# Nine modulation vectors as row products: transposed weights times a spread c, summed by VectorE, loaded by GpSimd's queue

## The chip, the cores and the metric

One core of a Trainium2 chip runs the whole kernel. The metric is the device time of one execution in microseconds; of several executions the median is given. The engines are TensorE (matrix products, PE in the profile; PEld is its weight load), VectorE (DVE), ScalarE (ACT), GpSimd (POOL) and SyncE (SP, which here only issues transfers). Each has its own queue and takes its instructions in order. Transfers run on 16 DMA engines that all queues share.

## What is computed

A trunk of two layers on 256 positions of width 2048: layer 0 is an RWKV-7 time mixing with a squared-ReLU MLP, layer 1 a chunked band attention with another such MLP. Every sub-layer is modulated by vectors made from one conditioning vector c:

```python
for layer in range(DEPTH):
    mod = c @ w_ada[layer] + b_ada[layer]
    sh1, sc1, gt1, sh2, sc2, gt2 = jnp.split(mod, 6, axis=-1)
    if layer == N_A_LAYERS:
        sh_kv, sc_kv = jnp.split(c @ w_ada_kv + b_ada_kv, 2, axis=-1)
        h_kv = modulate(rms_norm(x, g_kv), sh_kv, sc_kv)
        k_s, v_s = h_kv @ w_k_shared, h_kv @ w_v_shared
    h = modulate(rms_norm(x, g_mix[layer]), sh1, sc1)
    y = rwkv7_time_mix(h, ...) if layer < N_A_LAYERS else chunk_band_attention(h, kp, vp, ...)
    x = x + gt1 * y
    h = modulate(rms_norm(x, g_mlp[layer]), sh2, sc2)
    x = x + gt2 * sq_relu_mlp(h, w_up[layer], w_down[layer])
return rms_norm(x, g_final)
```

There are 6 + 6 + 2 = 14 modulation vectors of 2048 elements, each c (2048) times a matrix of 2048 x 2048: 16 MB of weights for each, read once, two operations for each weight. `(layer, part)` names a vector: parts 0 and 1 are the first shift and scale, 2 the first gate, 3 and 4 the second shift and scale, 5 the second gate; `("kv", 0)` and `("kv", 1)` are the shift and scale of the shared keys and values.

## The kernel before

**Layout.** Activations lie with the feature on the 128 partitions and the 256 positions in the row: `x` is [128, 16, 256]. Vectors lie as [128, 16], a column for each 128 features.

**The large products.** Every weight matrix is taken in blocks of 128 output columns (16 for width 2048). `weight` loads such a block in two halves of [128, 1024] (512 KB each) into `raw` (6 buffers, SP's queue); `halves` cuts each into a rounded part wH (ScalarE, L378) and the rest wL (VectorE, L381), with three buffers of each. `proj2` then takes 16 pairs of products (L412, L413) for a block, into `pj`. Behind a block VectorE adds up the two sums, or adds them to x (L960, L1016, L945).

**The modulation vectors.** (0,0) and (0,1) are made at the start, in a way of their own: the lower half of c as products on TensorE, the upper half as rows, L696, with `crow`, the upper half of c, spread over the partitions. The other twelve are made a step at a time beside the large products, in the order of `ada_tiles`: for each vector two halves of 1024 output columns, for each half 16 tiles of [128, 1024], one for each 128 elements of c, 384 tiles in all. `ada_step` takes one tile: VectorE multiplies it with the c of its partition and adds it to `acc` (L452 for the first, L454 for the other 15; `acc` has one buffer). Behind the 16th, `ada_sum` sums `acc` over the partitions: 32 products with a column of ones on TensorE (L476), and VectorE adds the bias (L480). `fin` runs these right away, as `lazy` is never set.

**When steps are taken.** `ada(n)` takes n steps and then calls `ada_fill`. In the time mixing it is called in three slots of four from the third pair of heads on (111 tiles, loaded into `raw`, one at a time); in the MLPs behind every block, one and two steps in turn (`ada_tick`); in the attention one step behind a key block, two behind a value block, one or two behind a query block; in the attention's output projection one step for each of the first ten blocks. `ada_need` takes whatever is missing when a vector is wanted. In the MLPs and the attention the tiles have a pool of their own, `rada` (`ada_room`: 5 buffers in the MLPs, 3 in the attention), and `ada_fill` keeps one load less than that ahead. All loads, those of `rada` too, are issued from SP's queue (L368), each behind the wait for its buffer.

**Order.** The program is written in one order; a scheduler then places each engine's instructions, by this order and by its own estimate of when each is ready, so that modulation steps may be placed ahead of instructions that were written before them. `tc.issue_after(i)` keeps what is written in its block, on the engine of i, behind i. GpSimd's own work in the later stages is the sum of squares (L518) and the masks of the scores (L1095, L1096).

Of the kernel before, what the change touches and what calls it, by code (L numbers as in the profile page):

```python
# [12 lines left out]
F32 = mybir.dt.float32  # L13
F32R = mybir.dt.float32r
AF = mybir.ActivationFunctionType
ALU = mybir.AluOpType
AX = mybir.AxisListType

P = 128
D = 2048  # L20
T = 256
KT = D // P
# [8 lines left out]
HK = 8  # L31
# [298 lines left out]
class Body:  # L330
# [27 lines left out]
            self.ada_pool = None  # L358

    def raw(self, src, shape=None, ada=False):  # L360
        if ada and self.ada_pool:
            pool, n = self.ada_pool
            t = pool.tile([P, HK * P], F32, tag="rada", bufs=n, name="rada")
        else:
            t = self.wp.tile([P, HK * P], F32, tag="raw", bufs=self.RAW_BUFS, name="raw")
        if shape is not None:
            t = t.rearrange("p (a b) -> p a b", a=shape)
        self.nc.sync.dma_start(out=t, in_=src)  # L368
        return t

    def halves(self, raw, lo=0):
# [47 lines left out]

    def ada_src(self, layer, part):  # L420
        if layer == "kv":
            at, w = 2 * 96 + 16 * part, self.d["w_ada_kv"]
        else:
            at, w = 96 * layer + 16 * part, self.d["w_ada"][layer]
        return w[:, part * D:(part + 1) * D], self.bada[:, at:at + KT]

    def ada_tiles(self):
        for key in [(0, 2), (0, 4), (0, 3), (0, 5), ("kv", 1), ("kv", 0),
                    (1, 1), (1, 0), (1, 2), (1, 4), (1, 3), (1, 5)]:
            for half in range(KT // HK):  # L430
                for kt in range(KT):
                    yield key, half, kt

    def ada_load(self):
        tile_ = next(self.adas, None)
        if tile_ is not None:
            key, half, kt = tile_
            w, n_ = self.ada_src(*key)[0], HK * P
            raw = self.raw(w[kt * P:(kt + 1) * P, half * n_:(half + 1) * n_], ada=True)
            self.ada_q.append((key, half, kt, raw))  # L440
        return tile_ is not None

    def ada_step(self):
        nc = self.nc
        if not (self.ada_q or self.ada_load()):
            return
        key, half, kt, raw = self.ada_q.popleft()
        ck = self.ct[:, kt:kt + 1]
        if kt == 0:
            self.fin(HK)  # L450
# [4 lines left out]
        if kt == KT - 1:  # L455
            self.fins = self.ada_sum(self.acc, self.mods[key], half, self.ada_src(*key)[1])
            if not self.lazy:
                self.fin(HK)
            if half == KT // HK - 1:
                self.ada_done.add(key)  # L460

    def ada_fill(self):
# [22 lines left out]
            next(self.fins, None)  # L485

    def ada(self, n=1):
        for _ in range(n):
            self.ada_step()
        self.ada_fill()  # L490

    def last_pe(self):
        pe = self.nc.tensor.engine
        return next(i for i in reversed(self.nc.cur_bb.bb.instructions) if i.engine == pe)

    def ada_need(self, *keys):
        while not all(k in self.ada_done for k in keys):
# [76 lines left out]
    def run(self):  # L574
        nc, tc, d = self.nc, self.tc, self.d
        ctx = self.ctx
        gp = self.gp = ctx.enter_context(tc.tile_pool(name="gp", bufs=1))
# [14 lines left out]
            self.mods[(0, part)] = self.mods01[:, part, :]  # L592
        self.nhalf, self.pool_every = 0, 0
        self.lazy, self.fins, self.ada_pool = False, iter(()), None
        self.ada_done = set()
        self.adas, self.ada_q = self.ada_tiles(), deque()

# [2 lines left out]
        with ExitStack() as st:  # L600
# [21 lines left out]
            with ExitStack() as s2:  # L622
# [4 lines left out]
                r = self.rstd()  # L627
# [535 lines left out]
def _arrange(x, c, w_ada, b_ada, g_mix, g_mlp, w_up, w_down,  # L1163
# [5 lines left out]
    f = lambda a: np.ascontiguousarray(np.asarray(a))  # L1169
    w_ada = f(w_ada)  # L1170
# [9 lines left out]
    for i, w in ((0, rwkv_w2), (1, rwkv_a2)):  # L1180
        w = f(w)[0]
# [17 lines left out]
        "b_ada": f(np.concatenate([f(b_ada).reshape(-1), f(b_ada_kv).reshape(-1)]).reshape(-1, P).T),  # L1199
        "w_ada0": f(w_ada[0][:HK * P, :2 * D]),  # L1200
        "w_ada0_t": f(w_ada[0][HK * P:, :2 * D].T).reshape(2 * KT, P, HK * P),
        "w_ada": f(w_ada), "w_ada_kv": f(w_ada_kv),
        "w_up": np.stack([_pack(w) for w in f(w_up)]),
        "w_down": np.stack([_pack(w) for w in f(w_down)]),
        "w_r": _pack(f(rwkv_w_r)[0]), "w_k": _pack(f(rwkv_w_k)[0]), "w_v": w_v,
# [26 lines left out]
```

## Time and profile before

| | |
|---|---|
| three runs | 2665.96, 2665.98, 2670.43 us; median 2665.98 |
| profiled execution | 2668.82 us, of which the span of its instructions is 2667.0 us |
| mean granted TensorE clock | 0.992 |
| read from memory | 656.72 MB, 247 GB/s over the span |
| loads into `rada` | 273 of 512 KB |

A page of the profile gives busy times of each engine, the costliest groups of instructions (line, engine, operation, what is written and read, shape, count, busy time and mean), transfers with the time from issue to landing, and waits with what ended them. Rows in order of time begin with the start in us and the duration in us. In the table by stage each engine's busy time stands with the number of its instructions, then the granted clock, the DMA engines' share and GB/s. The stages are, roughly: start and time mixing to 710 us, its output projection to 780, the first MLP to 1515, the attention to 1840, its output projection to 1940, the second MLP to the end.

### The profile page before, as it was taken

Reading aid. Unit: us, or ns where it says so; the run is one execution under the profiler, and the core shown is the slowest. Engines: PE = TensorE matmul, PEld = TensorE weight load, DVE = VectorE, ACT = ScalarE, POOL = GpSimd, SP = SyncE. Lnnn points to the kernel's source line nnn. Section 1 sums busy time; section 2 is a strip of 40 time slices with the busy share of each in tenths; the row PEclk is TensorE's granted clock in tenths of the full one; section 3 lists DMA queues with packets and bytes.
Section 4 is the critical chain, followed back from the end, with each engine's and each line's share of the span. In section 5 each row is a group of like instructions: output and inputs, shape, how many; then the busy total and the mean of one; then the engine's idle time right before and its main releaser. Section 6 shows DMA issues by size and latency. Waiting matters only on the chain.

```text
span 2667.0 us, 58173 instructions
## 1 busy us (share of the span) xinstructions
PE 2594.2 (97%) x23596; PEld 2229.2 (84%) x23596; DVE 2112.8 (79%) x3102; ACT 1345.2 (50%) x2435; POOL 208.7 (8%) x320
## 2 busy tenths in 40 slices
PE   7999999999999999999999999999999999999997
PEld 4787777887899888888888998877898888888886
DVE  6788888889789888888888898899887555555555
ACT  3346455555456445355365554565564463453554
POOL 0002223322110000000001100000100000000002
PEclk9999999999999999999999999999999999999998
DMA  9976556566778888889898679887766555555553
GB/s 349 312 244 211 185 179 207 180 214 199 246 236 312 309 317 327 319 324 332 318 329 293 238 242 331 318 274 256 265 218 235 190 189 184 188 189 186 186 189 119
DMA packets 207149, 662.62 MB, mean 248 GB/s; under 512 B 21408, under 2 KB 54560, under 8 KB 206880
## 3 DMA queue, kind: packets, MB, share of 16 engines
q1 hardware_dynamic: 204816, 656.36, 71.5%
q8 instruction: 185, 3.03, 0.5%
q10 hardware_dynamic: 2064, 2.54, 0.3%
q14 instruction: 84, 0.69, 0.1%
HBM read 656.72 MB, written 2.10 MB: 247 GB/s over the span
## 4 chain that ended last, share of the span: by engine, by line
PE 85%; DVE 5%; issue 4%; DMA 4%; ACT 2%; POOL 1%; DVEq 0%; SPq 0%; ACTq 0%; POOLq 0%
PE pj L412 45%; PE pj L413 23%; PE pj L402 2%; PE pj L401 2%; PE pj L403 2%; DMA raw<-w_ada 1%; DVE wL L381 1%; PE iv L111 1%; DVE acc L454 1%; PE gr L105 1%; ACT wH L378 1%; PE ms L115 1%; PE o L401 1%; PE ms L324 0%; PE ms L105 0%
## 5 line engine op out<-in xcount | busy, mean ns | idle before, releaser
L381 DVE TENSOR_TENSOR wL<-raw,wH 128x1024 fp32r<-128x1024 f32 x772 | 941.1, 1220 | 354.9 <-ACT wH L378 347.0
L378 ACT CAST wH<-raw 128x1024 fp32r<-128x1024 f32 x772 | 805.8, 1045 | 799.7 <-PE pj L412 650.0
L412 PE MATMUL pj<-aHL,wH 128*128 128x512 f32 x3328 | 1202.0, 403 | 1.9 <-DVE x L945 1.4
L413 PE MATMUL pj<-aHL,wL 128*128 128x256 f32 x3328 | 936.1, 281 | 0.4 <-DVE wL L381 0.4
L412 PEld LDWEIGHTS pj<-aHL,wH 128*128 128x128 f32 x3328 | 629.4, 189 | 154.4 <-issue 8.7
L412 PE MATMUL pj<-hHL,wH 128*128 128x512 f32 x2048 | 723.0, 398 | 0.0
L413 PEld LDWEIGHTS pj<-aHL,wL 128*128 128x128 f32 x3328 | 629.4, 189 | 3.1 <-issue 0.8
L413 PE MATMUL pj<-hHL,wL 128*128 128x256 f32 x2048 | 574.4, 281 | 0.0
L412 PEld LDWEIGHTS pj<-hHL,wH 128*128 128x128 f32 x2048 | 384.6, 188 | 94.4 <-DVE hHL L991 0.2
L413 PEld LDWEIGHTS pj<-hHL,wL 128*128 128x128 f32 x2048 | 386.8, 189 | 0.1
L454 DVE SCALAR_TENSOR_TENSOR acc<-rada,ct,acc 128x1024 f32<-128x1024 f32 x256 | 327.2, 1278 | 8.5 <-DMA rada<-w_ada 7.6
L518 POOL TENSOR_TENSOR ss<-ss,sq 128x256 f32<-128x256 f32 x56 | 52.6, 940 | 1590.8 <-ACT sq L517 1590.5
L1016 DVE SCALAR_TENSOR_TENSOR x<-pj,mod,x 128x256 f32<-128x256 f32 x256 | 123.4, 482 | 58.6 <-PE pj L413 54.9
L454 DVE SCALAR_TENSOR_TENSOR acc<-raw,ct,acc 128x1024 f32<-128x1024 f32 x104 | 136.2, 1309 | 15.3 <-DMA raw<-w_ada 14.9
L988 ACT ACTIVATE t<-t 128x256 f32<-128x256 f32 x112 | 46.8, 418 | 123.5 <-DVE t L960 123.5
L401 PE MATMUL pj<-aHL,wH 128*128 128x258 f32 x384 | 109.0, 284 | 0.0
L402 PE MATMUL pj<-aHL,wH 128*128 128x258 f32 x384 | 108.9, 284 | 0.0
L403 PE MATMUL pj<-aHL,wL 128*128 128x258 f32 x384 | 108.0, 281 | 0.0
L403 PEld LDWEIGHTS pj<-aHL,wL 128*128 128x128 f32 x384 | 73.2, 191 | 0.2
L402 PEld LDWEIGHTS pj<-aHL,wH 128*128 128x128 f32 x384 | 72.6, 189 | 0.1
L401 PEld LDWEIGHTS pj<-aHL,wH 128*128 128x128 f32 x384 | 72.2, 188 | 0.2
L990 ACT ACTIVATE t<-t 128x256 f32<-128x256 f32 x128 | 53.4, 417 | 3.4
(249 smaller groups left out, 2815.5 us busy)
## 6 DMA issues: line engine op xcount, KB each, us to landing
raw<-w_up SPq DMA_DIRECT2D x256, 512.0 KB, 4.2
raw<-w_down SPq DMA_DIRECT2D x256, 512.0 KB, 4.3
rada<-w_ada SPq DMA_DIRECT2D x209, 512.0 KB, 5.8
raw<-w_ada SPq DMA_DIRECT2D x111, 512.0 KB, 4.3
rada<-w_ada_kv SPq DMA_DIRECT2D x64, 512.0 KB, 6.1
rawa<-w_ada SPq DMA_DIRECT2D x32, 512.0 KB, 6.9
rawa<-w_ada_t SPq DMA_DIRECT2D x32, 512.0 KB, 7.5
raw<-w_k SPq DMA_DIRECT2D x32, 512.0 KB, 4.0
```

Of the source, the lines that this page charges most:

```text
L378: nc.scalar.copy(Hf, raw)
L381: eng.tensor_tensor(out=Lf, in0=raw, in1=Hf, op=ALU.subtract)
L401: nc.tensor.matmul(ps, H[:, i, :], a(kt)[:, 0, :], start=(first and kt == 0), stop=False)
L402: nc.tensor.matmul(ps, H[:, i, :], a(kt)[:, 1, :], start=False, stop=False)
L403: ins = nc.tensor.matmul(ps, L[:, i, :], a(kt)[:, 0, :], start=False, stop=(last and kt == KT - 1))
L412: nc.tensor.matmul(ps, H[:, i, :], a(kt), start=(kt == 0), stop=False)
L413: ins = nc.tensor.matmul(ps[:, 0, :], L[:, i, :], a(kt)[:, 0, :], start=False, stop=(kt == KT - 1))
L454: nc.vector.scalar_tensor_tensor(out=self.acc, in0=raw, scalar=ck, in1=self.acc, op0=ALU.mult, op1=ALU.add)
L518: (eng or nc.gpsimd).tensor_tensor(out=self.ss, in0=self.ss, in1=sq, op=ALU.add)
L988: nc.scalar.activation(t, t, AF.Relu)
L990: nc.scalar.activation(t, t, AF.Square)
L1016: nc.vector.scalar_tensor_tensor(out=x, in0=ps[:, i, :], scalar=self.mods[(layer, 5)][:, n:n + 1], in1=x, op0=ALU.mult, op1=ALU.add)
```

## The change

Three vectors, (0,2), (0,4) and (0,3), are made as before. The other nine, from (0,5) on, are made from transposed weights (`w_ada_t`, laid out outside the kernel): a tile is 128 output features by one half (1024) of c, contiguous in memory. `ada_row` multiplies it in place with `cb`, that half of c spread over the 128 partitions, and the same VectorE instruction sums the row into one column of the vector, for the first half of c, or of `sums`, for the second. Behind 16 tiles one addition on VectorE adds the bias (first half) or the sums (second half). TensorE takes no part. There are as many tiles as before, 288 for the nine vectors, and the order of the halves is such that `cb` changes its half five times behind the first load: first halves and second halves of several vectors are taken together. `cb` takes the buffer of `acc` and is loaded by SP's queue.

Loads into `rada` are issued from GpSimd's queue instead of SP's; loads into `raw` stay with SP. Where there is a `rada`, `ada` keeps its steps behind the last VectorE instruction written so far.

```diff
--- before.py
+++ after.py
@@ -358,14 +358,16 @@
             self.ada_pool = None
 
     def raw(self, src, shape=None, ada=False):
+        queue = self.nc.sync
         if ada and self.ada_pool:
             pool, n = self.ada_pool
+            queue = self.nc.gpsimd
             t = pool.tile([P, HK * P], F32, tag="rada", bufs=n, name="rada")
         else:
             t = self.wp.tile([P, HK * P], F32, tag="raw", bufs=self.RAW_BUFS, name="raw")
         if shape is not None:
             t = t.rearrange("p (a b) -> p a b", a=shape)
-        self.nc.sync.dma_start(out=t, in_=src)
+        queue.dma_start(out=t, in_=src)
         return t
 
     def halves(self, raw, lo=0):
@@ -419,32 +421,49 @@
 
     def ada_src(self, layer, part):
         if layer == "kv":
-            at, w = 2 * 96 + 16 * part, self.d["w_ada_kv"]
+            at, first = 2 * 96 + 16 * part, KT * (7 + part)
         else:
-            at, w = 96 * layer + 16 * part, self.d["w_ada"][layer]
-        return w[:, part * D:(part + 1) * D], self.bada[:, at:at + KT]
+            at, first = 96 * layer + 16 * part, KT * (1 + part if layer else 0)
+        if layer == 0 and part < 5:
+            w = self.d["w_ada"][:, (part - 2) * D:(part - 1) * D]
+        else:
+            w = self.d["w_ada_t"][first:first + KT]
+        return w, self.bada[:, at:at + KT]
 
     def ada_tiles(self):
-        for key in [(0, 2), (0, 4), (0, 3), (0, 5), ("kv", 1), ("kv", 0),
-                    (1, 1), (1, 0), (1, 2), (1, 4), (1, 3), (1, 5)]:
+        for key in [(0, 2), (0, 4), (0, 3)]:
             for half in range(KT // HK):
                 for kt in range(KT):
-                    yield key, half, kt
+                    yield key, half, kt, None
+        e, f, g = (0, 5), ("kv", 1), ("kv", 0)
+        p, q, r, s, t, u = [(1, i) for i in (1, 0, 2, 4, 3, 5)]
+        seen = set()
+        for half, keys in enumerate([[e], [e, f, g], [f, g, p, q], [p, q, r, s, t], [r, s, t, u], [u]]):
+            for key in keys:
+                for n in range(KT):
+                    yield key, half % 2, n, key in seen
+                seen.add(key)
 
     def ada_load(self):
         tile_ = next(self.adas, None)
         if tile_ is not None:
-            key, half, kt = tile_
+            key, half, kt, last = tile_
             w, n_ = self.ada_src(*key)[0], HK * P
-            raw = self.raw(w[kt * P:(kt + 1) * P, half * n_:(half + 1) * n_], ada=True)
-            self.ada_q.append((key, half, kt, raw))
+            if last is None:
+                raw = self.raw(w[kt * P:(kt + 1) * P, half * n_:(half + 1) * n_], ada=True)
+            else:
+                raw = self.raw(w[kt, half], ada=True)
+            self.ada_q.append((key, half, kt, last, raw))
         return tile_ is not None
 
     def ada_step(self):
         nc = self.nc
         if not (self.ada_q or self.ada_load()):
             return
-        key, half, kt, raw = self.ada_q.popleft()
+        key, half, kt, last, raw = self.ada_q.popleft()
+        if last is not None:
+            self.ada_row(key, half, kt, last, raw)
+            return
         ck = self.ct[:, kt:kt + 1]
         if kt == 0:
             self.fin(HK)
@@ -459,6 +478,23 @@
             if half == KT // HK - 1:
                 self.ada_done.add(key)
 
+    def ada_row(self, key, half, n, last, raw):
+
+        nc = self.nc
+        if self.cb_half != half:
+            n_, self.cb_half = HK * P, half
+            self.fin(HK)
+            self.cb = self.wp.tile([P, n_], F32, tag="acc", bufs=1, name="cb")
+            nc.sync.dma_start(out=self.cb, in_=self.d["c_row"][0:1, half * n_:(half + 1) * n_].to_broadcast([P, n_]))
+        dst, bias = self.mods[key], self.ada_src(*key)[1]
+        sums = self.sums if last else dst
+        nc.vector.scalar_tensor_tensor(out=raw, in0=raw, scalar=1.0, in1=self.cb, op0=ALU.mult, op1=ALU.mult,
+                                       accum_out=sums[:, n:n + 1])
+        if n == KT - 1:
+            nc.vector.tensor_tensor(out=dst, in0=dst, in1=self.sums if last else bias, op=ALU.add)
+            if last:
+                self.ada_done.add(key)
+
     def ada_fill(self):
         while self.ada_pool and len(self.ada_q) < self.ada_pool[1] - 1 and self.ada_load():
             pass
@@ -485,13 +521,17 @@
             next(self.fins, None)
 
     def ada(self, n=1):
-        for _ in range(n):
-            self.ada_step()
+        nc = self.nc
+        with self.tc.issue_after(self.last_on(nc.vector)) if self.ada_pool else nullcontext():
+            for _ in range(n):
+                self.ada_step()
         self.ada_fill()
 
+    def last_on(self, eng):
+        return next(i for i in reversed(self.nc.cur_bb.bb.instructions) if i.engine == eng.engine)
+
     def last_pe(self):
-        pe = self.nc.tensor.engine
-        return next(i for i in reversed(self.nc.cur_bb.bb.instructions) if i.engine == pe)
+        return self.last_on(self.nc.tensor)
 
     def ada_need(self, *keys):
         while not all(k in self.ada_done for k in keys):
@@ -592,6 +632,8 @@
             self.mods[(0, part)] = self.mods01[:, part, :]
         self.nhalf, self.pool_every = 0, 0
         self.lazy, self.fins, self.ada_pool = False, iter(()), None
+        self.cb_half = None
+        self.sums = gp.tile([P, KT], F32, name="ada_sums")
         self.ada_done = set()
         self.adas, self.ada_q = self.ada_tiles(), deque()
 
@@ -1199,7 +1241,9 @@
         "b_ada": f(np.concatenate([f(b_ada).reshape(-1), f(b_ada_kv).reshape(-1)]).reshape(-1, P).T),
         "w_ada0": f(w_ada[0][:HK * P, :2 * D]),
         "w_ada0_t": f(w_ada[0][HK * P:, :2 * D].T).reshape(2 * KT, P, HK * P),
-        "w_ada": f(w_ada), "w_ada_kv": f(w_ada_kv),
+        "w_ada": f(w_ada[0][:, 2 * D:5 * D]), "c_row": f(c).reshape(1, D),
+        "w_ada_t": f(np.concatenate([w.T for w in (w_ada[0][:, 5 * D:], w_ada[1], np.asarray(w_ada_kv))], 0)
+                     .reshape(9 * KT, P, 2, HK * P).transpose(0, 2, 1, 3)),
         "w_up": np.stack([_pack(w) for w in f(w_up)]),
         "w_down": np.stack([_pack(w) for w in f(w_down)]),
         "w_r": _pack(f(rwkv_w_r)[0]), "w_k": _pack(f(rwkv_w_k)[0]), "w_v": w_v,
```

## The prediction, made before the result was known

> **What bounds the kernel now.** I read the page's busy shares first, then the table by stage, then TensorE's and VectorE's waits, then VectorE's order of time.
>
> ```profile
> span 2667.0 us, 58173 instructions
> PE 2594.2 (97%) x23596; PEld 2229.2 (84%) x23596; DVE 2112.8 (79%) x3102; ACT 1345.2 (50%) x2435; POOL 208.7 (8%) x320
> ```
>
> The table by stage (window, its length, busy time of each engine, granted clock, DMA share, GB/s) shows where this holds:
>
> ```profile
> core 0: us, PE busy (x) PEld busy (x) DVE busy (x) ACT busy (x) POOL busy (x), PEclk, DMA share, GB/s
> 200.00:700.00 500.00, 478.81 (x9481) 395.79 (x9480) 432.26 (x796) 262.87 (x723) 129.27 (x178) 0.99 0.61 199
> 780.00:980.00 200.00, 200.00 (x1427) 179.18 (x1426) 182.05 (x234) 99.99 (x145) 0.00 (x0) 1.00 0.84 303
> 980.00:1180.00 200.00, 200.00 (x1376) 173.66 (x1375) 167.48 (x196) 100.67 (x150) 0.00 (x0) 1.00 0.87 318
> 1180.00:1400.00 220.00, 220.00 (x1431) 191.26 (x1431) 194.49 (x222) 111.94 (x167) 0.00 (x0) 1.00 0.91 325
> 1400.00:1600.00 200.00, 200.00 (x1378) 179.79 (x1377) 178.02 (x248) 107.27 (x159) 14.06 (x24) 1.00 0.75 257
> 1600.00:1800.00 200.00, 199.37 (x1386) 165.49 (x1386) 174.77 (x283) 106.18 (x223) 4.69 (x40) 1.00 0.87 307
> 1800.00:2030.00 230.00, 227.67 (x1610) 198.38 (x1608) 204.30 (x311) 129.41 (x232) 13.01 (x28) 1.00 0.74 253
> ```
>
> From 780 us to 2030 us, the stretch in which nearly all the changed work lies, TensorE is idle for 0.63 + 2.33 = 3 us of 1250. VectorE is second: its six rows add up to 1101 us, 88%, so 149 us are free. The DMA engines are third, at 253 to 325 GB/s. So time is won only by taking instructions off TensorE, and lost only when VectorE or a transfer comes so late that TensorE runs dry.
>
> **Term 1: the sums on TensorE go.** Each half of a vector ends in 32 products of `acc` with a column of ones (L476), which the trace records as 64. The group's row, and one such place in TensorE's order of time:
>
> ```profile
> L476 PE MATMUL m<-csts,acc x1152: 170/170/191, 817.2 to 2023.1; 128*32 128x1 f32 x192
> 816.85 0.28 PE L402 MATMUL pj<-aHL,wH 128*128 128x258 f32 x1
> 816.96 0.28 PE L403 MATMUL pj<-aHL,wL 128*128 128x258 f32 x1
> 817.17 0.71 PE L476 MATMUL m<-csts,acc 128*32 128x1 f32 x64
> 817.81 0.39 PE L401 MATMUL pj<-aHL,wH 128*128 128x258 f32 x1
> ```
>
> 1152 / 64 = 18 halves, that is the nine vectors that the change turns to rows, and all lie between 817 and 2023 us. Neighbouring products start 816.96 - 816.85 = 0.11 to 0.12 us apart; with the sum between, the next one starts 817.81 - 816.96 = 0.85 us later. So a half costs 0.85 - 0.12 = 0.73 us of TensorE, and 18 x 0.73 = **-13.1 us**. The vectors (0,2), (0,4), (0,3) keep their sums.
>
> **Term 2: VectorE's work.** Old and new form both occur in the trace; what counts is the distance from one start to the next.
>
> ```profile
> 869.49 0.74 DVE L452 TENSOR_SCALAR acc<-rada,ct 128x1024 f32<-128x1024 f32 x1
> 870.15 0.42 DVE L960 TENSOR_TENSOR t<-pj,t 128x256 f32<-128x256 f32 x1
> 871.62 1.28 DVE L454 SCALAR_TENSOR_TENSOR acc<-rada,ct,acc 128x1024 f32<-128x1024 f32 x1
> 872.82 0.41 DVE L991 TENSOR_TENSOR hHL<-t,hHL 128x256 fp32r<-128x256 f32 x1
> 40.06 1.22 DVE L696 SCALAR_TENSOR_TENSOR rawa<-rawa,crow 128x1024 f32<-128x1024 f32 x1
> 41.21 0.08 DVE L696 DVE_READ_ACCUMULATOR rawa<-rawa,crow 128x1 f32 x1
> 41.21 0.42 DVE L572 TENSOR_TENSOR aHL<-mix,aHL 128x256 fp32r<-128x256 f32 x1
> ```
>
> An accumulating step holds VectorE for 872.82 - 871.62 = 1.20 us, the first of a half 870.15 - 869.49 = 0.66 us. The row product of the first stage, the same instruction as the new one, holds it for 41.21 - 40.06 = 1.15 us; reading its accumulator (0.08 us) runs beside the next instruction. Before: 270 x 1.20 + 18 x 0.66 = 336 us; after: 288 x 1.15 = 331 us. The closing additions are two per vector both times. VectorE is relieved by about 5 us and loses its wait for TensorE's sums; as TensorE sets the pace, I book 0.
>
> **Term 3: the spread c.** `cb` has one buffer (the tag of `acc`) and changes at row tiles 0, 16, 64, 128, 208 and 272, six times. Each new load waits on SP's queue until the last product has read the old half, with weight loads behind it, and the next product waits for its landing, with everything behind it on VectorE. VectorE's own rows show what such a stall may last. Two neighbouring blocks of w_down in which no modulation step falls:
>
> ```profile
> 914.80 1.00 DVE L1016 SCALAR_TENSOR_TENSOR x<-pj,mod,x 128x256 f32<-128x256 f32 x2 [0.64 <-PE pj L413]
> 915.76 1.22 DVE L381 TENSOR_TENSOR wL<-raw,wH 128x1024 fp32r<-128x1024 f32 x1
> 918.59 1.23 DVE L381 TENSOR_TENSOR wL<-raw,wH 128x1024 fp32r<-128x1024 f32 x1 [1.60 <-ACT wH L378]
> 920.45 1.00 DVE L1016 SCALAR_TENSOR_TENSOR x<-pj,mod,x 128x256 f32<-128x256 f32 x2 [0.64 <-PE pj L413]
> ```
>
> A block is 920.45 - 914.80 = 5.65 us. Three buffers of wH and wL mean that the first half for the block after next is cut while TensorE is in the next one. With the new order the one or two modulation steps come right behind the block's x additions: 0.96 + 2 x 1.15 + 1.15 = 4.4 us until that wL is done, so in a full block 1.2 us are spare, and with one step 2.4 us. The landing is bounded by these rows (KB each, median us):
>
> ```profile
> rada<-w_ada SPq DMA_DIRECT2D x209, 512.0 KB, 5.8
> rada<-w_ada_kv SPq DMA_DIRECT2D x64, 512.0 KB, 6.1
> raw<-w_o SPq DMA_DIRECT2D x4, 128.0 KB, 2.4
> ```
>
> `cb` writes 512 KB too, but reads 4 KB of memory over and over. Landing in 2.4 us costs nothing; in 6 us, with all of VectorE held, 6 - 1.2 = 5 us. As a rule other work stands ahead of the waiting product (wL of weights long loaded), so I take 0.6 us for each of the five changes behind 700 us, **+3 us**, and keep 0 and +25. The first change falls into the tail of the time mixing, where the row above has TensorE at 479 of 500 us already; **+0.5**, bounds 0 and +5.
>
> **Term 4: loads from GpSimd's queue.** 209 + 64 = 273 loads leave SP, which has nothing to win by it: TensorE's waits between 780 and 2030 us name no transfer,
>
> ```profile
> PE pj L412 <- DVE x L945: 1.4, 1, 1.4
> PE pT L1120 <- DVE s L1109: 0.5, 2, 0.3
> PE pj L413 <- DVE wL L381: 0.4, 1, 0.4
> ```
>
> and VectorE's wait for `rada` is small:
>
> ```profile
> DVE acc L454 <- DMA rada<-w_ada: 7.1, 11, 2.7
> ```
>
> GpSimd has room (4.69 to 14.06 us busy in the stage rows), and its own work behind a waiting load, the squares' sums and the score masks, is needed blocks later. What counts is lateness, where VectorE must take the steps in order. In the MLPs four loads are ahead, some 15 us at 1.5 steps a block: hidden. In the attention's value projections only two are, and two steps are taken in every block:
>
> ```profile
> 1619.66 0.42 DVE L960 TENSOR_TENSOR vf<-pj,vf 128x256 f32<-128x256 f32 x1
> 1625.50 0.42 DVE L960 TENSOR_TENSOR vf<-pj,vf 128x256 f32<-128x256 f32 x1
> L223 POOL TENSOR_TENSOR al<-da,csts 128x512 f32<-128x512 f32 x16 | 18.5, 1157 | 0.0
> ```
>
> A block there is 5.84 us. The load into the buffer that the first step frees must land before the second step of the next block, 5.84 + 1.15 = 7.0 us on. From SP it took 5.8 to 6.1. The trace has no load issued by GpSimd; I bound its extra by nothing and by GpSimd's longest instruction, 1.16 us. Even then 6.0 + 1.2 = 7.2 against 7.0 is inside the spare of about 1 us. I book **+1.5 us** over the 16 blocks, bounds 0 and +32 (2 us a block). The Trainium skill (DMA: Bandwidth & Descriptors, Specifications) puts the first byte of a GpSimd load at about 1 us against 0.6 us from SP; by that difference, an estimate of 0.4 us, the load would be in time and the term nearer 0.
>
> **The pinned order.** The new `issue_after` in `ada` keeps a product behind the last VectorE instruction of its block. Before, steps were taken in bursts (none between 914.80 and 920.45 above), so the same work is spread more evenly, without a cost of its own; the contiguous source leaves each load at 512 KB. Both 0.
>
> **Sum,** on the profiled execution's 2668.82 us (span 2667.0 and 1.8 around it): 2668.8 - 13.1 + 3 + 0.5 + 1.5 = 2660.7. That execution stood 2.84 us over the median of the three, 2665.98; on that scale **2658 us**, 0.3% faster.
>
> **Rivals.**
> - *Late loads (slower).* Loads by GpSimd need 9 us or more from the freed buffer; then in the value projections each block waits about 2 us, in order, and wL behind it comes late. 16 x 2 = 32 us: 2666 - 13 + 32 + 3 = **2688 us**. It decides from a lateness of 1.2 us a block. For it: two loads ahead only, and 307 GB/s there. Against: the small wait for `rada` today.
> - *GpSimd and VectorE block each other (slower).* The squares' sums show that they can:
>
> ```profile
> 1433.52 0.74 POOL L518 TENSOR_TENSOR ss<-ss,sq 128x256 f32<-128x256 f32 x1 [659.89 <-ACT sq L517]
> 1433.56 1.77 DVE L381 TENSOR_TENSOR wL<-raw,wH 128x1024 fp32r<-128x1024 f32 x1
> 1437.24 1.22 DVE L381 TENSOR_TENSOR wL<-raw,wH 128x1024 fp32r<-128x1024 f32 x1
> ```
>
>   Beside GpSimd's sum wL took 1.77 us, alone 1.22. If making a load held VectorE up by 0.55 us, 273 x 0.55 = 150 us would use up the 149 free, and TensorE would wait wherever the load is above the mean, I estimate a tenth of it: 2666 - 13 + 5 + 15 = **2673 us**. The Trainium skill (SBUF — State Buffer, Who interferes with whom) says that a VectorE instruction with two SBUF inputs collides only with GpSimd work that reads SBUF, and infers that writing descriptors does not; by that rule this rival falls and the forecast stands. No row here shows such a load.
> - *The spread c stalls in full (slower).* 5 us at five places, +25: 2666 - 13 + 25 + 2 = **2680 us**, from landings above 4 us with nothing ahead of the product.
> - *No change.* Small stalls of about 2 us a change and 0.3 us a value block eat the saving: **2665 us**.
>
> **Chances.** Forecast 0.50, late loads 0.16, blocking 0.10, stalled c 0.11, no change 0.13. A difference under 0.2% (5.3 us) can't be told from none here. The forecast's own range is 2652 to 2662; a twentieth of it falls within 0.2%. Faster: 0.50 less that and plus a little of the others, 0.51; same: 0.13 + 0.03 + a few of the rivals at half price, 0.18; slower 0.31. For 8 in 10 the range reaches down to the bare term 1 with 2 us spare, 2651, and up to the late loads, 2688.
>
> **What would show it.** Right: no L476 after 780 us, TensorE still at 100% between 780 and 2030, the stage some 10 us shorter, product and next instruction 1.15 us apart. Term 3 wrong: VectorE waiting several us for `cb` with TensorE waiting for wL behind it. Term 4 wrong: VectorE waiting for `rada` in the value projections, loads of 8 us. Blocking: wL's mean above its present 1.22 us where GpSimd loads. The whole is wrong if TensorE's idle time in that stretch grows by more than 13 us.

## The result and the profile after

The changed kernel is slower: 2682.12 us median of six executions (2678.96 to 2690.16) against 2667.8 us for the kernel before, measured beside it (six, 2665.96 to 2671.03); ratio 1.0057, 95% interval 1.0044 to 1.0071. The profiled execution took 2678.96 us, 3.2 us under its median. The head of its page, and the table by stage over the same windows as before:

```profile
span 2677.2 us, 56146 instructions
PE 2579.9 (96%) x22444; PEld 2217.3 (83%) x22444; DVE 2104.6 (79%) x3390; ACT 1340.7 (50%) x2435; POOL 357.8 (13%) x593
```

```profile
780.00:980.00 200.00, 197.68 (x1252) 178.07 (x1251) 175.16 (x272) 99.84 (x145) 22.21 (x42) 1.00 0.85 295
980.00:1180.00 200.00, 198.05 (x1125) 172.16 (x1124) 171.73 (x252) 99.72 (x149) 27.98 (x53) 1.00 0.92 325
1180.00:1400.00 220.00, 217.88 (x1244) 190.10 (x1244) 188.95 (x277) 112.00 (x170) 30.61 (x58) 1.00 0.92 327
1400.00:1600.00 200.00, 198.48 (x1253) 178.80 (x1252) 179.96 (x278) 108.68 (x162) 27.76 (x50) 1.00 0.77 262
1600.00:1800.00 200.00, 197.11 (x1198) 163.77 (x1196) 174.80 (x334) 105.46 (x224) 30.97 (x90) 1.00 0.86 304
1800.00:2030.00 230.00, 223.03 (x1402) 194.87 (x1402) 201.63 (x345) 126.74 (x231) 36.02 (x67) 0.99 0.78 259
```

TensorE has 2594.2 - 2579.9 = 14.3 us less to do, as intended. But its idle time between 780 and 2030 us grew from 3 to 17.8 us (the six rows add up to 1232.2 of 1250): by 14.8 us, more than the 13 that the prediction named as the sign that the whole is wrong. Over the whole span it grew by 24.5 us; some 4 us of that lie between 2030 and 2300 us and as much ahead of 780. The span is 10.2 us longer: -14.3 + 24.5. What TensorE waits for between 700 and 2060 us, and what VectorE waits for (waiting instruction, releaser, us in total, times, longest):

```profile
PE pj L415 <- DVE wL L383: 16.2, 10, 3.6
PE o L405 <- DVE wL L383: 5.1, 4, 2.1
```

```profile
DVE rada L491 <- DMA cb<-c_row: 19.6, 5, 4.8
...
DVE rada L491 <- DMA rada<-w_ada_t: 14.5, 12, 3.2
```

In `proj2`, TensorE's wait for wL went from 0.4 to 16.2 us, and VectorE, which makes wL, waits for the spread c and for row tiles. The groups of the new work and of wL, and the transfers' rows:

```profile
L383 DVE TENSOR_TENSOR wL<-raw,wH 128x1024 fp32r<-128x1024 f32 x772 | 937.3, 1220 | 353.6 <-ACT wH L380 350.8
L491 DVE SCALAR_TENSOR_TENSOR rada<-rada,cb 128x1024 f32<-128x1024 f32 x273 | 327.8, 1220 | 34.5 <-DMA cb<-c_row 19.6
L370 POOL DMA_DIRECT2D rada<-w_ada_t x273 | 145.2, 532 | 980.4 <-DVE rada L491 877.7
rada<-w_ada_t POOLq DMA_DIRECT2D x273, 512.0 KB, 6.1
```

```profile
L488 SPq DMA_DIRECT2D cb<-c_row x6: 327/328/328, 677.7 to 1986.4; - x6
DMA to landing us min/median/max: 5.0/7.7/8.0
```

The second fence is the view of the tile `cb`: six loads, landing 5.0 to 8.0 us after their issue. The last one with the two plain loads issued within 1.2 us behind it (KB each, us to landing), its issue in SP's order of time, and what VectorE does meanwhile:

```profile
cb<-c_row SPq DMA_DIRECT2D x1, 512.0 KB, 7.7
rada<-w_ada_t POOLq DMA_DIRECT2D x1, 512.0 KB, 7.6
raw<-w_up SPq DMA_DIRECT2D x1, 512.0 KB, 7.8
```

```profile
1986.40 0.33 SPq L488 DMA_DIRECT2D cb<-c_row  x1
```

```profile
1986.29 1.23 DVE L383 TENSOR_TENSOR wL<-raw,wH 128x1024 fp32r<-128x1024 f32 x1
...
1989.08 1.23 DVE L383 TENSOR_TENSOR wL<-raw,wH 128x1024 fp32r<-128x1024 f32 x1 [1.14 <-ACT wH L380]
1994.22 1.23 DVE L491 SCALAR_TENSOR_TENSOR rada<-rada,cb 128x1024 f32<-128x1024 f32 x1 [3.90 <-DMA cb<-c_row]
...
1995.70 1.22 DVE L491 SCALAR_TENSOR_TENSOR rada<-rada,cb 128x1024 f32<-128x1024 f32 x1
...
1997.19 1.22 DVE L383 TENSOR_TENSOR wL<-raw,wH 128x1024 fp32r<-128x1024 f32 x1
```

The load is issued at 1986.40, when the last product with the old half has ended. Two wL stand ahead of the waiting product, and they are done 3.9 us before the load lands; the next wL starts 1997.19 - 1989.08 = 8.1 us after the second, in a stretch where a block, with two wL, takes 5.6 us. The plain loads issued behind it land late too, against 6.1 us for the row tiles at the median. Some 30 us later, ahead of the first block of the second w_down, vector (1,5) is wanted and what is missing of it is taken at once:

```profile
2021.42 1.23 DVE L491 SCALAR_TENSOR_TENSOR rada<-rada,cb 128x1024 f32<-128x1024 f32 x1 [3.19 <-DMA rada<-w_ada_t]
...
2022.90 2.35 DVE L383 TENSOR_TENSOR wL<-raw,wH 128x1024 fp32r<-128x1024 f32 x2
2025.17 0.42 DVE L1033 TENSOR_TENSOR hHL<-t,hHL 128x256 fp32r<-128x256 f32 x1
2025.51 1.22 DVE L491 SCALAR_TENSOR_TENSOR rada<-rada,cb 128x1024 f32<-128x1024 f32 x1
...
2032.99 1.23 DVE L491 SCALAR_TENSOR_TENSOR rada<-rada,cb 128x1024 f32<-128x1024 f32 x1 [1.00 <-DMA rada<-w_ada_t]
2034.14 0.08 DVE L491 DVE_READ_ACCUMULATOR rada<-rada,cb 128x1 f32 x1
2034.25 1.23 DVE L491 SCALAR_TENSOR_TENSOR rada<-rada,cb 128x1024 f32<-128x1024 f32 x1
2035.40 1.22 DVE L383 TENSOR_TENSOR wL<-raw,wH 128x1024 fp32r<-128x1024 f32 x1
```

Seven row products lie between two wL: from 2025.17 to 2035.40 VectorE makes no wL. Just ahead of them a row product has waited 3.19 us for its tile, with wL behind it. In the trace of before the last sum of (1,5) was closed at 2023.86, since its scheduler had put steps into VectorE's gaps earlier:

```profile
2023.86 0.16 DVE L480 TENSOR_TENSOR mod<-m,bada 128x8 f32<-128x8 f32 x1
```

To size each place, I set the same product side by side in several traces: the first products of `proj2` (the line that writes `pj` from wH, 16 to a block) are counted from the start, and the time between two of them is compared. So only what moves TensorE's products shows in it. Two columns are runs told of below: the pinned steps and GpSimd's queue with the old arithmetic, and the changed kernel with one spread.

```
products     where                               before  old arithm.  changed  one spread
464-512      time mixing's end to first MLP      143.33    144.23     147.94    146.65
1152-1200    change of cb, issued at 1005.5       16.82     16.82      18.99     16.82
1840-1872    change of cb, issued at 1245.3       11.31     11.09      13.96     11.09
2800-2816    change of cb, issued at 1635.9        5.83      5.84       7.65      5.84
3520-3552    change of cb, issued at 1986.4       11.21     11.21      13.23     11.21
3552-3648    catch-up ahead of (1,5)              34.37     37.75      45.50     41.42
```

Against the old arithmetic in the same order, the four late changes of `cb` cost 2.17 + 2.87 + 1.81 + 2.02 = 8.9 us of TensorE, the catch-up 7.8 us, the stretch up to the first MLP 3.7 us. At the change issued at 826.7 us the count shows less than 1 us. At 14 of the 18 places of a removed sum the changed kernel gains 0.73 or 0.74 us on the kernel before, at three others 0.64 to 1.9; the last place lies in the catch-up.

### The profile page after: what moved, and what is told of

Same layout as the page of the kernel before. It is cut to its first block, busy times and chain, and to the rows that moved or that the text cites. A ratio compares the mean times of both kernels' runs of the same rounds, so it can differ in the third digit from the quotient of the medians.

```text
span 2677.2 us, 56146 instructions
## 1 busy us (share of the span) xinstructions
PE 2579.9 (96%) x22444; PEld 2217.3 (83%) x22444; DVE 2104.6 (79%) x3390; ACT 1340.7 (50%) x2435; POOL 357.8 (13%) x593
## 3 DMA queue, kind: packets, MB, share of 16 engines
q0 software_dynamic: 39312, 143.15, 15.6%
## 4 chain that ended last, share of the span: by engine, by line
PE 75%; issue 9%; DVE 8%; DMA 4%; ACT 2%; POOL 1%; DVEq 0%; POOLq 0%; ACTq 0%; SPq 0%
PE pj L414 39%; PE pj L415 20%; DVE wL L383 2%; PE pj L404 2%; PE pj L403 2%; PE pj L405 2%; DMA raw<-w_ada 1%; DVE acc L473 1%; DVE rada L491 1%; ACT wH L380 1%; PE iv L111 1%; POOL rada L370 1%; DMA cb<-c_row 1%; DMA rada<-w_ada_t 1%; PE gr L105 1%
## 5 line engine op out<-in xcount | busy, mean ns | idle before, releaser
L383 DVE TENSOR_TENSOR wL<-raw,wH 128x1024 fp32r<-128x1024 f32 x772 | 937.3, 1220 | 353.6 <-ACT wH L380 350.8
L491 DVE SCALAR_TENSOR_TENSOR rada<-rada,cb 128x1024 f32<-128x1024 f32 x273 | 327.8, 1220 | 34.5 <-DMA cb<-c_row 19.6
L370 POOL DMA_DIRECT2D rada<-w_ada_t x273 | 145.2, 532 | 980.4 <-DVE rada L491 877.7
L473 DVE SCALAR_TENSOR_TENSOR acc<-raw,ct,acc 128x1024 f32<-128x1024 f32 x90 | 118.2, 1313 | 19.5 <-DMA raw<-w_ada 19.2
L1030 ACT ACTIVATE t<-t 128x256 f32<-128x256 f32 x112 | 46.7, 417 | 155.3 <-DVE t L1002 155.3
```

The costliest lines, as they stand in the source:

```text
L370: queue.dma_start(out=t, in_=src)
L383: eng.tensor_tensor(out=Lf, in0=raw, in1=Hf, op=ALU.subtract)
L473: nc.vector.scalar_tensor_tensor(out=self.acc, in0=raw, scalar=ck, in1=self.acc, op0=ALU.mult, op1=ALU.add)
L491: nc.vector.scalar_tensor_tensor(out=raw, in0=raw, scalar=1.0, in1=self.cb, op0=ALU.mult, op1=ALU.mult, accum_out=sums[:, n:n + 1])
```

## The experiments

Theory: the sums on TensorE are worth what was predicted, and VectorE gives it back, at the changes of `cb` and in the catch-up that the pinned order brings. Rivals: GpSimd's queue is at fault; the pinned order alone is at fault. Each run's ratio is to the kernel before, run beside it, with its 95% interval.

**One spread.** The nine vectors are made with the first half of c in place of the second as well.

```diff
-        if self.cb_half != half:
+        if self.cb_half is None:
```

> The changed kernel, but the spread c is loaded once and never changed (the second half of every row product uses the first half of c, so the second half of c is left out of the nine vectors). Theory of stalls (VectorE waits for the spread at each of the five later changes and TensorE runs dry by about 2 us each): about 10 us faster than the changed kernel, 2672 us, and no wait of VectorE for cb behind 700 us. Rival, GpSimd's loads: no more than 2 us faster, 2680 us. The 11 us lost near 2025 to 2045 us stay by the theory, since that place has another cause (the catch-up before (1,5) is wanted).

2666.2 us, ratio 0.9991 (0.9982 to 1.0): more than I gave it. Its column above shows where: the four changes are back at 16.82, 11.09, 5.84 and 11.21 us, and the catch-up gave 4.1 us too. There VectorE's longest wait for a row tile (2000 to 2025 us) is 1.1 us in place of 3.2; that the stall at 1986 brought the longer one about is likely, but not shown. So the changes cost what the count says, and about 16 us with their consequences.

**One and two steps in turn in the attention's output projection**, in place of one a block, which leaves fewer steps for the second MLP.

```diff
-                    self.ada()
+                    self.ada(1 + n % 2)
```

> The changed kernel with one and two modulation steps in turn, instead of one, behind each of the first ten blocks of the attention's output projection: five more steps are done before the second MLP, so none has to be caught up before (1,5) is wanted. Theory of the catch-up: TensorE's 11 us lost near 2025 to 2045 us shrink below 2, the run takes about 2671 us. Rival, late loads from GpSimd's queue in the second MLP: VectorE still waits for rada there and most of the 11 us stay, about 2680 us. Rival, VectorE too full in the output projection: the loss moves there, about 2680 us.

2673.49 us, ratio 1.0021 (1.0012 to 1.003). Products 3552 to 3648 take 34.06 us in place of 45.50; but 4.6 us are lost in the output projection. The last change of `cb` has moved there with the steps (issued at 1906.76; VectorE waits 2.39 us for it), and its 2.0 us at products 3520 to 3552 are gone. The catch-up is a cost of its own, and what the moved steps cost is in good part the moved change.

**Loads from SP.** The row tiles loaded by SP again, the rest as changed.

```diff
             pool, n = self.ada_pool
-            queue = self.nc.gpsimd
```

> The changed kernel with the loads into rada issued from SP's queue as before the change. If GpSimd's queue costs time (blocking or lateness), this is faster than the changed kernel by 5 us or more, 2677 us or less. By the theory of stalls the queue has no share: 2680 to 2684 us, or slower, as on SP the load of the spread and the weights stand behind loads that wait for a row product.

2723.41 us, ratio 1.0203 (1.0185 to 1.022): far outside both. ScalarE's and SP's waits between 1060 and 1340 us:

```profile
ACT wH L379 <- DMA raw<-w_down: 81.0, 34, 6.6
...
ACT wH L379 <- DMA raw<-w_up: 27.8, 12, 4.0
```

```profile
SPq L369 <- DVE rada L490: 166.0, 57, 7.6
```

SP stands up to 7.6 us before a row load whose buffer is still in use, and the weight loads behind it come late: wH waits for them. By the count, the first MLP (products 512 to 2432, with the output projection's end) takes 38.6 us longer than in the changed kernel, spread over about a third of its blocks. With the new arithmetic GpSimd's queue is worth 41 us, and the rival that it is at fault falls.

**Not pinned.** The steps placed by the scheduler again.

```diff
-        with self.tc.issue_after(self.last_on(nc.vector)) if self.ada_pool else nullcontext():
+        with nullcontext():
```

> The changed kernel without issue_after around the modulation steps. If the pinned order costs time of itself, the steps drift ahead into VectorE's gaps as before the change, nothing is left to catch up in the second MLP, and the run takes 2671 us or less. Rival: the pin is needed, since a row product placed early waits for its load with wL behind it: slower than the changed kernel, 2690 us or more. The stalls at the changes of the spread, 10 us, stay by both.

2684.01 us, ratio 1.0059 (1.0045 to 1.0072). The catch-up is gone (33.80 us) and more is lost elsewhere: against the changed kernel 6.6 us between 777 and 836 us, and 14.4 between 1306 and 1438. In 1300 to 1430 us VectorE waits 4.7 us for `cb`, whose change has moved there, and 11.3 for row tiles, and TensorE 8.4 for the wL behind. The pinning isn't the fault by itself either; undoing it only moves the loss.

Three runs put the parts of the change on the kernel before, one or two at a time.

**Before, pinned.**

```diff
-        for _ in range(n):
-            self.ada_step()
+        nc = self.nc
+        with self.tc.issue_after(self.last_on(nc.vector)) if self.ada_pool else nullcontext():
+            for _ in range(n):
+                self.ada_step()
...
```

> The kernel before, with its old sums on TensorE and its loads from SP, and only the order of the steps pinned to their blocks. Theory (pinning takes away the steps made ahead, and the weight loads on SP then stand in line behind row loads that wait for a free buffer): the catch-up ahead of (1,5) costs about 11 us and the first MLP some 30 to 40 more, as in the run with loads from SP: 2710 to 2720 us. Rival (the line on SP comes only with the longer stalls of the spread c): 2675 to 2682 us, the catch-up alone.

2666.51 us, ratio 0.9995 (0.9984 to 1.0006). Both expectations missed: there is no line on SP here, and products 3552 to 3648 take 36.23 us, 1.9 more than before. VectorE's order of time shows why:

```profile
2027.34 1.28 DVE L454 SCALAR_TENSOR_TENSOR acc<-rada,ct,acc 128x1024 f32<-128x1024 f32 x1
2028.53 1.22 DVE L381 TENSOR_TENSOR wL<-raw,wH 128x1024 fp32r<-128x1024 f32 x1
2029.67 1.28 DVE L454 SCALAR_TENSOR_TENSOR acc<-rada,ct,acc 128x1024 f32<-128x1024 f32 x1
2030.87 0.48 DVE L1020 SCALAR_TENSOR_TENSOR x<-pj,mod,x 128x256 f32<-128x256 f32 x1
```

The old steps are caught up here too, but from 2024 us on the scheduler has set a wL or an addition to x between any two of them, while row products stand side by side. Why it places the two forms differently, the runs don't show.

**Before, with GpSimd's queue.**

```diff
             t = pool.tile([P, HK * P], F32, tag="rada", bufs=n, name="rada")
+            self.nc.gpsimd.dma_start(out=t, in_=src)
+            return t
```

> The kernel before, and only its row loads moved to GpSimd's queue. Theory (the queue is worth something only where the steps are pinned; the scheduler of before already places the loads where a buffer is free): 2665 to 2671 us, no change. Rival (GpSimd's queue is better wherever the loads are, the 41 us of the run with loads from SP being a price of SP): 2640 to 2655 us. Second rival (GpSimd asks too late without the pinned order, its own masks and adds ahead of the loads): 2680 us and more.

2682.92 us, ratio 1.0051 (1.0039 to 1.0063): the second rival. Its rows of the first MLP and of the stretch where the value projections end, and below them the same two of before:

```profile
780.00:1600.00 820.00, 819.30 (x5613) 724.09 (x5612) 722.02 (x898) 420.70 (x620) 110.39 (x207) 1.00 0.85 302
1650.00:1730.00 80.00, 73.39 (x462) 61.36 (x463) 63.59 (x76) 32.44 (x53) 12.71 (x24) 0.96 0.91 319
```

```profile
780.00:1600.00 820.00, 820.00 (x5606) 723.88 (x5605) 722.03 (x897) 419.87 (x619) 14.06 (x24) 1.00 0.84 301
1650.00:1730.00 80.00, 79.37 (x529) 66.84 (x529) 70.48 (x101) 40.64 (x77) 0.92 (x8) 1.00 0.90 320
```

In the 820 us with the first MLP the queue costs 0.7 us; between 1650 and 1730 TensorE idles 6.6 us in place of 0.6. There two loads only are ahead, and VectorE waits 15.6 us in all for row tiles (1600 to 1740 us, longest 4.0). The count of products puts 11.7 us of the loss between 1645 and 1740 us.

**Before, pinned and with GpSimd's queue**, that is both edits above: the changed kernel's order without its arithmetic.

> The kernel before with its old sums on TensorE, its row loads on GpSimd's queue and its steps pinned: the changed kernel's order without its arithmetic. Theory (the queue costs 14 us only where the scheduler moves the steps away from their blocks; pinned, it asks in time, and the catch-up ahead of (1,5) costs 2 us as in the pinned kernel of before): 2666 to 2671 us, so that the spread c alone takes more than the 13.1 us that the sums leave. Rival (queue and order add up whatever the arithmetic is): 2680 to 2684 us, as the changed kernel, the removed sums then being worth nothing against it.

2667.62 us, ratio 0.9994 (0.9985 to 1.0003): the theory. Queue and order do not add up: pinned, VectorE's waits for row tiles between 1640 and 1740 us fall to 2.2 us, and the queue costs nothing. This is the base to measure the arithmetic against: the arithmetic makes the kernel 2682.1 - 2667.6 = 14.5 us slower, although TensorE is rid of 13.1 us.

The last five change when steps are taken. In three, `cb` is loaded for the other half as soon as a vector's sixteen products are done, and the next call takes no step (`hold`; `owed` counts the steps to make up, and a call makes up one of them at most). A part of that edit:

```diff
+            if self.ada_pool and self.ada_q and self.ada_q[0][1] != half:
+                self.cb_load(1 - half)
+                self.hold = 1
...
-            for _ in range(n):
+                for _ in range(min(n + 1, self.owed)):
```

**The hold alone.**

> The other half of c is loaded as soon as a vector's sixteen row products are done, and the next call takes no step, so that a block's work covers the landing; the steps owed are made up one at a time. Theory (the changes of cb cost 2.0 to 2.8 us each because the first row product of the new half is asked for at once): no wait of VectorE for cb at the four changes inside the MLP and the projections behind it, and 2682.1 - 8 = about 2674 us; the tail ahead of the closing add of (1,5) stays. Rival (the 7.7 us of landing is only the sign of a busy stretch, and the block that makes up the owed step pays as much): 2681 to 2683 us.

2679.09 us, ratio 1.0039 (1.0027 to 1.0051), between the two. Three changes go by without a wait, two keep one. SP's order of time with the two loads, and VectorE's with the products that wait for them:

```profile
1241.97 0.33 SPq L502 DMA_DIRECT2D cb<-c_row  x1
...
1636.87 0.33 SPq L502 DMA_DIRECT2D cb<-c_row  x1
```

```profile
1249.62 1.23 DVE L489 SCALAR_TENSOR_TENSOR rada<-rada,cb 128x1024 f32<-128x1024 f32 x1 [3.18 <-DMA cb<-c_row]
...
1644.76 1.23 DVE L489 SCALAR_TENSOR_TENSOR rada<-rada,cb 128x1024 f32<-128x1024 f32 x1 [5.22 <-DMA cb<-c_row]
```

The held call covered (1249.62 - 3.18) - 1241.97 = 4.5 us of the first and 2.7 us of the second, less than a landing. And the steps owed end in the catch-up: products 3552 to 3648 take 46.48 us. In the profiled executions the hold wins nothing between products 512 and 3648 (1319.39 us, changed 1318.03).

**The rate alone**: in both MLPs 13 steps more in 20 ticks in place of 10, that is 1.65 steps a block in place of 1.5.

```diff
-        self.nticks = getattr(self, "nticks", 0) + 10
+        self.nticks = getattr(self, "nticks", 0) + 13
```

> The changed kernel with 13 in place of 10 steps more in 20 ticks of the first MLP and nothing else: the new half of c is still loaded at its first row product. Theory (the stalls at the changes, about 9 us, and the catch-up ahead of (1,5), about 11 us, add up, and each edit takes one of them): the tail goes, the waits for cb stay: about 2671 us. Rival (only the rate matters, since VectorE catches a stall up where it isn't behind with steps): 2659 to 2663 us. Second rival (more steps in the first MLP cost TensorE there): 2676 us and more.

2671.03 us, ratio 1.0012 (1.0001 to 1.0023), as the theory had it. VectorE's wait for `cb` is nearly all there, and products 3552 to 3648 take 33.50 us:

```profile
DVE rada L491 <- DMA cb<-c_row: 16.8, 5, 4.1
```

**Hold and rate, the first half of c loaded early**, when (0,3) is done.

> The hold, and 13 steps more in 20 ticks of the first MLP in place of 10, so that little or nothing is left to catch up ahead of the closing add of (1,5), and the first half of c is loaded when the last key of the old form is done. Theory: the changes give back 8 us, the tail up to 11, the first load 2 to 3: about 2660 us, below both kernels. Rival (VectorE has no room for more steps in the first MLP, as the two steps per block of the output projection gave back 4 us there): 2668 to 2672 us.

**Hold and rate, the first half loaded as in the changed kernel.**

> The hold and the 13 in 20 ticks of e15, but the first half of c loaded where the changed kernel loads it, at its first row product. Theory (the 4 to 6 us lost by 740 us do not come from the first load of c, since e15 has them too): 2657 to 2661 us, as e15. Rival (the early load gave its 2 to 3 us and something else took them): 2661 to 2664 us.

2658.66 us, ratio 0.9968 (0.9956 to 0.998), and 2660.08 us, ratio 0.996 (0.9947 to 0.9974): both are faster than the kernel before and the changed one, and alike, so the early load gives nothing. Against the changed kernel the hold alone gives 3 us, the rate alone 11 and both 22: with the rate, the hold is worth 2671.0 - 2660.1 = 11 us. Five stages of the second, and TensorE's wait for wL between 700 and 2060 us:

```profile
780.00:980.00 200.00, 199.96 (x1257) 179.72 (x1257) 178.38 (x278) 101.05 (x145) 23.66 (x44) 1.00 0.85 300
...
1180.00:1400.00 220.00, 220.00 (x1263) 192.94 (x1263) 197.79 (x292) 114.94 (x173) 33.94 (x65) 1.00 0.96 346
1400.00:1600.00 200.00, 197.23 (x1247) 177.75 (x1246) 181.19 (x283) 107.45 (x159) 27.55 (x53) 1.00 0.78 267
1600.00:1800.00 200.00, 197.95 (x1211) 164.89 (x1210) 176.84 (x336) 105.75 (x226) 30.93 (x92) 1.00 0.87 305
1800.00:2030.00 230.00, 229.75 (x1454) 202.01 (x1454) 195.06 (x327) 130.90 (x233) 26.81 (x49) 1.00 0.72 235
```

```profile
PE pj L415 <- DVE wL L383: 3.0, 4, 1.4
```

With the sums gone, TensorE is nearly full again: it idles 5.1 us from 780 to 2030 us, 2.8 of them between 1400 and 1600. From product 512 to 3648 this kernel takes 1295.05 us; before takes 1313.04, the changed kernel 1318.03. The 4.9 us that it gains beyond the sums lie between 1750 and 1850 us, where the pinned kernels with the old arithmetic gain as much and lose it elsewhere. Ahead of product 512 it loses ground: 464 to 512 take 149.38 us, 5 more than with the old arithmetic, and the early load doesn't change that (150.33).

**Before, with the rate alone**, the same edit of the ticks as above: the control.

> The kernel before with 13 in place of 10 steps more in 20 ticks, its sums on TensorE: the control for the other two. Theory (before has no catch-up to lose, since its steps already stand in VectorE's gaps): 2665 to 2670 us. Rival (the rate is a gain of its own, with which the row form has nothing to do): 2655 to 2662 us.

2698.11 us, ratio 1.0109 (1.0095 to 1.0123). Both expectations missed, on the slow side. It loses some 31 us between 950 and 1490 us, up to 2.7 us a block, where TensorE waits for wL again and again (28 times, 19.7 us in all between 700 and 2060 us). I didn't follow this further. With the scheduler's order the rate is no gain by itself; the old arithmetic pinned, with GpSimd's queue and this rate, wasn't run, so what the rate would give there is open. That the two fast kernels owe their gain to the new arithmetic rests on the count: no sum of the nine vectors is left, and about 0.73 us are gained where each stood.

## Why the prediction was wrong

It said 2658 us, faster; it was 2682.1, slower. Two steps failed, the price of the spread c and the pinned order that was booked at nothing. The wide range up to 2688 held the time only by an end that was set for another cause, late loads.

- **Bound of the kernel: right.** TensorE sets the pace, and most of the time was lost where wL came late.
- **Term 1, -13.1 us: right.** 0.73 us at nearly each of the 18 places, and no such sum left behind 780 us.
- **Term 2, 0: right in its rows.** The row product's pitch is 1.15 us in the rows above (2034.25 to 2035.40 for one product), and its mean 1220 ns as in the first stage.
- **Term 3, +3 us for the spread c: mis-sized.** The step that failed is "as a rule other work stands ahead of the waiting product, so I take 0.6 us". Other work did stand ahead, two wL at each of the four changes from 1005 us on, but it was done 3.8 to 4.8 us before the landing. Landing took 7.7 us at the median, above the 6 us that I had taken as its upper bound; that was a median of plain loads, and even plain loads took 7.6 to 9.4 us when issued right behind `cb` at these changes. Measured: 8.9 us at these four, 0.9 at the one from 826.7, and about 4 more in the catch-up that follows the last one; the run with one spread has them gone. The mechanism was named, and its bound of +25 held it.
- **The first change, +0.5 us: too small, cause open.** The stretch that holds it is 3.7 us longer than with the old arithmetic. The run with one spread has the same first load, so it can't test this; its 146.65 us shows how far two executions with the same work here may differ. VectorE's own wait for this load is 0.2 us, and an early load gives nothing. The first fifteen row products end 8 us later than the old steps did; what that costs isn't settled.
- **The pinned order, 0: the other step that failed.** "The same work is spread more evenly, without a cost of its own" left out that steps made ahead are lost, and that `ada_need` then makes up the rest at one point, with wL behind it. In the old arithmetic that costs 2 to 3 us (34.37 to 36.23 and 37.75), with row products 11 (45.50). Of these 11, the 4 named under term 3 go with the spread too, and 3.2 us of VectorE's wait for a row tile lie in the stretch; with one spread it costs 7 (41.42). The run with more steps a tick takes 11 us off, as expected of it.
- **Term 4, GpSimd's queue: right in size, wrong in its reason.** In the pinned order with the old arithmetic it costs nothing. But "SP has nothing to win by it" fell: with row products SP's queue loses 41 us. The sign that I had named, VectorE waiting for `rada` in the value projections, did show: 8.8 us between 1640 and 1740 us in the changed kernel, for 1.6 us of TensorE by the count. Where the order isn't pinned it is worse, 6.0 us of TensorE's idle time between 1650 and 1730. In the two pinned kernels with the old arithmetic the 209 loads from `w_ada` land in 5.3 us at the median from SP and in 5.8 from GpSimd. The Trainium skill (DMA: Bandwidth & Descriptors, Specifications) puts GpSimd's first byte about 0.4 us behind SP's; the 0.5 here agrees.
- **The rival of blocking engines: fell.** wL's mean is 1220 ns with 273 loads made by GpSimd, and 1220 without. The Trainium skill (SBUF — State Buffer, Who interferes with whom) infers that writing descriptors doesn't hold a VectorE instruction of this kind; the two means agree with that.
- **The rival of the stalled c, 2680 us, came nearest,** in part by luck: the stalls cost about half of its 25 us, and the catch-up, which it doesn't have, made up the rest.

The ledger of the profiled executions against the pinned kernel with the old arithmetic: -13.1 + 3.7 + 8.9 + 7.8 = 7.3 us, or 8.0 if the last of the 18 sums, which the 7.8 already holds, isn't counted twice; their spans differ by 2677.2 - 2668.2 = 9.0. What else the count shows is 1.4 us ahead of product 464, 0.9 and 1.9 at 834 and 874 us, and -2.9 behind product 3648. The medians differ by 14.5, since the profiled execution of the changed kernel stands 3.2 us under its median and the other 2.3 over its own. Single executions do scatter: product 464 comes after 584.7 to 592.7 us in the fourteen profiled ones, where no kernel has reached a row product yet. What makes this scatter isn't shown, and the stretch up to product 512 may hold some of it.

## What to carry to other kernels

Where one engine sets the pace and another feeds it in order, a buffer that changes its contents is priced by the landing of the load less the work that is ahead of it in that engine's own queue. Take the landing from a load of the same kind at such a place, not from the median of others; load the next contents as soon as the last reader is done and leave that engine other work meanwhile. When steps are tied to their blocks, count what is still owed at each point that needs a result, since it is paid there at once. And measure queue, order and arithmetic together as well as apart: here the queue alone cost 14 us, the order alone nothing, both nothing, and the arithmetic gave 8 us of its 13 only after the rate and the loads were fitted to it.

## What the runs showed of the hardware that I had not expected

A row of 4 KB spread over 128 partitions lands later than most plain loads of 512 KB: 7.5 to 8.0 us at the five changes behind 800 us, while the row tiles in the same execution take 6.1 at the median and one in ten of those far from a change 7.5 or more. The plain loads issued within 1.7 us behind it land late too, in 7.5 to 9.4 us. Whether the spread load holds them up or the moment is a busy one isn't shown; in the run with loads from SP it takes 6.3 at the median and the row tiles 5.2. Making a 512 KB load occupies GpSimd for 532 ns, and 273 of them left VectorE's instructions as long as they were.
